# One 512-column matmul for the high and low parts of 256 tokens, and a gate/up evacuation in two pieces

## The chip, the cores and the metric

The kernel runs on one core of a Trainium2 chip. The metric is the device time of one launch in microseconds; the time before is the median of three runs.

The engines are named as the profile names them: PE is TensorE (PEld its weight loads), DVE is VectorE, ACT is ScalarE, POOL is GpSimd, SP the engine that issues the transfers. ps is a tile of PSUM, one bank of 512 float32 columns; blk, t, u, raw, whi and wlo are tiles in SBUF.

## The reference

Two transformer blocks on 256 tokens of 1024 features, in float32:

- Block 1: a modulation from a condition vector, RMS norm, one wide input projection, two attentions (sliding window and block), gates, an output projection, and an MLP `y = square(relu(h @ w_mlp_in)) @ w_mlp_out` of 4096 features, both with a gated residual.
- Block 2: 16 learned tokens are put in front (272 tokens). Layer 0: half a swiglu, a pooling mixer, half a swiglu. Layer 1, whose queries are the 256 tokens alone: half a swiglu, latent attention over shared keys and values, half a swiglu, and a last norm. A swiglu is

```python
def swiglu(h, w_gate, w_up, w_down):
    return (jax.nn.silu(h @ w_gate) * (h @ w_up)) @ w_down
```

with 2816 features between. So there are four swiglus: two of 272 tokens (layer 0) and two of 256 tokens (layer 1).

## The kernel before, in words

Activations are held with features on the 128 partitions and tokens along the columns. A matmul takes a 128 x 128 tile of weights as the stationary operand and streams the token columns.

**Precision.** Weights and activations are float32, each split exactly into two parts of the matmul type float32r: a high part and the rest. `mm3` (L116) makes one product of three matmuls: high weights by high activations (L119), high weights by low activations (L120), low weights by high activations (L121). Each loads its own stationary tile, so the high weights are loaded twice.

**Weights.** `ld` (L82) brings 1 MB (128 x 2048) by one transfer into one of three `raw` buffers and splits it in two halves of 1024 columns: the high part is a copy on ACT (L103), the low part a subtraction on DVE (L104). There are four `whi` and four `wlo` buffers of 1024 columns, so two loads are held at a time, and a split waits until PE is through with the buffer that it takes.

**Projections.** `proj` (L223) takes two feature tiles by step, with k over 8 input tiles: 2 x 8 x 3 matmuls. A step of a swiglu's gate/up projection makes one gate tile and one up tile of the 22. Behind each step its `evac` runs; the first steps' evacuations wait for the norm of the tokens. `down` (L628) is the second projection: four pairs of output tiles, each pair over all k (32 in the MLP, 22 in a swiglu), then `evac` for both.

**Evacuations.** In a swiglu (`ffn`, L689) `evac` (L696) scales the gate by the token norm (DVE, L698), applies Silu (ACT, L699), scales up (DVE, L701), multiplies the two (POOL, L702), and `split_act` takes the high part (ACT, L192) and the low part (DVE, L193). `devac` (L708) adds half of the result to the residual (DVE, L712) and calls what follows: `post_y` (L722) splits the sum for the next projection (L188, L189) and squares it for the norm (POOL, L200, L201). The last swiglu's `post_out` (L1068) makes a scaled copy on ACT (L1069) that PE transposes for the output. The MLP's evacuations are `mlp_evac` (L595) and `mlp_out_evac` (L646).

**Buffers.** High and low parts of an activation are separate tiles of eight features each, from one pool of 13 blocks. `PT` (L468, L999) are three buffers of 384 columns that the attentions use. PSUM has eight banks; a step takes two.

**Order.** Each engine works strictly in the order in which its instructions were emitted. That order is set by a scheduler of the framework, which goes by the order of the program and by its own estimate of when an instruction is ready; the kernel pins it at a few places (`issue_after`).

The 256-column products through `mm3` are: the block-1 projections, the MLP's down projection, and in layer 1 both swiglus, the query projections and the attention's output projection. The MLP's first projection has 258 columns (two carry the shift), layer 0 has 272.

Of the kernel before, what the change touches and what calls it, by code (L numbers as in the profile page):

```python
# [18 lines left out]
S = 256  # L19
# [10 lines left out]
# columns of the packed per-feature vectors  # L30
# [15 lines left out]
def net(ctx, tc, d):  # L46
# [35 lines left out]
    def ld(src, n, sub=1024, spare=False, pool=False, cut=False, steps=None, after=((), ())):  # L82
        """parts of a weight block; with steps, the part behind the first is left to a call of what is put there"""
        raw = wp.tile([128, 2048], F32, tag="raw", name=nm("raw"), bufs=3)
        for a, b in ((0, sub), (sub, n)) if cut else ((0, n),):
            with behind(order[:1]):
                i = nc.sync.dma_start(raw[:, a:b], src[:, a:b])
            if order:
                order[:1] = [i]
        parts = []  # L90
        if spare:
            bh, bl = blk([128, 2048], F32R), blk([128, 2048], F32R)

        def part(a):
            m = min(sub, n - a)
            if spare:
                hi, lo = bh[:, a:a + m], bl[:, a:a + m]
            else:
                hi = wp.tile([128, 1024], F32R, tag="whi", name=nm("whi"), bufs=4)
                lo = wp.tile([128, 1024], F32R, tag="wlo", name=nm("wlo"), bufs=4)  # L100
            e = G if pool and a else V
            with behind(after[a > 0]):
                i = A.activation(hi[:, :m], raw[:, a:a + m], AF.Copy)  # L103
                e.tensor_tensor(lo[:, :m], raw[:, a:a + m], hi[:, :m].bitcast(F32), op=OP.subtract)  # L104
            if order and not a:
                order[1:] = [i]
            parts.append((hi, lo))

        for a in range(0, n, sub):
            if a and steps is not None:  # L110
                steps.append(lambda a=a: part(a))
            else:
                part(a)
        return parts

    def mm3(out, w, c0, xh, xl, start, stop, m=128):  # L116
        """out += (whi + wlo).T (xhi + xlo), the weights stationary."""
        hi, lo = w
        TE.matmul(out, hi[:, c0:c0 + m], xh, start=start, stop=False, skip_group_check=True)  # L119
        TE.matmul(out, hi[:, c0:c0 + m], xl, start=False, stop=False, skip_group_check=True)  # L120
        TE.matmul(out, lo[:, c0:c0 + m], xh, start=False, stop=stop, skip_group_check=True)  # L121

# [88 lines left out]
    def sumsq_late(parts, src, f, n, sumsq=sumsq):  # L211
        """as sumsq, the last two tiles on their own: their squares are ready sooner."""
# [10 lines left out]
    def proj(src, evac, nj, n, yh, yl, first=2, hooks=(), at={}, orders=(range(0, 6), range(6, KD)), spare=(),  # L223
             after={}):
        """two feature tiles by step. The first steps take the tiles of y in the given order, with what is ready
        first in front; the hooks go behind each part of the order and behind the steps that follow, and only
        then the first sums are used. at[j] goes behind step j."""
        hooks = list(hooks)
        waiting = []

# [7 lines left out]
        def mms(pp, w, ks, tiles=(0, 1)):  # L238
            for k in ks:
                for i in tiles:  # L240
                    mm3(pp[i][:, 0:n], w[k // 4], (k % 4) * 256 + i * 128, yh[:, k, :], yl[:, k, :],
                        k == 0, k == KD - 1)
# [7 lines left out]
        for ks in orders:  # L250
# [7 lines left out]
            if len(orders) == 2:  # L258
                if ks[-1] == KD - 1:
                    waiting += [lambda j=j: evac(j, *pps[j]) for j in range(first)]  # L260
                hook()
        tight = len(orders) != 2
        if tight:
            waiting += [lambda j=j: evac(j, *pps[j]) for j in range(first)]
            hook()
        for j in range(first, nj):
            w = ld(src[j], 2048)
            if tight and j == first:
# [5 lines left out]
                evac(j, *pp)  # L274
# [3 lines left out]
            if waiting:  # L278
                waiting.append(lambda j=j, pp=pp: evac(j, *pp))
                hook()  # L280
            else:
                evac(j, *pp)
            if j in at:
                at[j]()

# [7 lines left out]
    def ada(ch, t0, t1, early=False):  # L293
        """feature tiles t0, t1 of the modulation: a row of ada_w.T per partition, times silu(c), summed."""
# [12 lines left out]
    def ada_rest(n, early=False):  # L307
        """n more chunks: gate1, scale2, shift2, gate2."""
# [22 lines left out]
    # position bias with its masks, as a Toeplitz table  # L331
# [50 lines left out]
    # q feature tiles (tokens back to front within each half), then k  # L382
# [25 lines left out]
    def scores(fam, half):  # L408
# [22 lines left out]
        if fam == 0:  # L431
            # heads i, i+4, i+1, i+5 of the sinks
# [24 lines left out]
    def values(fam, heads, Sb, rd, mid):  # L457
        PTs, po = [], []

        def tr(j):  # L460
# [7 lines left out]
            PTs.append(work([128, 384], "PT", bufs=3))  # L468
# [74 lines left out]
    # branches, merge  # L543
# [19 lines left out]
    # out projection, residual; y = x1 * g2 * (1 + scale2), with shift2 as two more columns  # L563
# [27 lines left out]
    # MLP  # L591
    ah = [blk([128, 8, S], F32R) for _ in range(4)]
    al = [blk([128, 8, S], F32R) for _ in range(4)]

    def mlp_evac(f, p):  # L595
# [8 lines left out]
        h = ah[f // 8][:, f % 8, :]  # L604
        A.activation(h, u, AF.Square)
        V.tensor_tensor(al[f // 8][:, f % 8, :], q, h.bitcast(F32), op=OP.subtract)
# [6 lines left out]
    # MLP out, residual; final norm of block 1 and first norm of block 2 both applied late  # L613
# [14 lines left out]
    def down(src, kcs, evac, n, ah, al, before=None):  # L628
        for dp in range(4):
# [3 lines left out]
            for c, (k0, nk) in enumerate(kcs):  # L633
                w = ld(src(dp, c), nk * 256)
                for kk in range(nk):
                    k = k0 + kk
                    for i in range(2):
                        mm3(pp[i][:, 0:n], w[kk // 4], (kk % 4) * 256 + i * 128, ah[k // 8][:, k % 8, :],
                            al[k // 8][:, k % 8, :], k == 0, k == kcs[-1][0] + kcs[-1][1] - 1)
# [6 lines left out]
    def mlp_out_evac(f, p):  # L646
        x2 = work([128, PADW], "t")[:, :S]
        V.scalar_tensor_tensor(x2, p[:, 0:S], mod[:, GA2 + f:GA2 + f + 1], x1[:, f, :], op0=OP.mult, op1=OP.add)
# [6 lines left out]
    down(lambda dp, c: d["mlp_out"][dp * 4 + c], [(8 * c, 8) for c in range(4)], mlp_out_evac, S, ah, al,  # L655
# [17 lines left out]
    def rms_of(get, tiles, n):  # L673
        """hooks that leave the norm of y's tokens in a row."""
# [14 lines left out]
    def ffn(idx, yh, yl, rms, h, n, c0, post, kv=False, before=None, **kw):  # L689
        """h[:, c0:] + half of the swiglu of y; post(f, h_f) for each feature tile of the sum."""  # L690
        gh = [blk([128, nk, n], F32R) for _, nk in FC]
        gl = [blk([128, nk, n], F32R) for _, nk in FC]
        hooks, rc = rms
        c1 = T - n if kv else 0

        def evac(f, pg, pu):  # L696
            g = work([128, PADW], "t")[:, :n]
# [10 lines left out]
        def devac(f, p):  # L708
            if f == 0:
                out.append(blk([128, KD, n]))  # L710
            hn = out[0]
            split[:] = [V.scalar_tensor_tensor(hn[:, f, :], p[:, 0:n], 0.5, h[:, f, c0:], op0=OP.mult, op1=OP.add)]  # L712
            post(f, hn[:, f, :])
# [5 lines left out]
    def make_y(n, y):  # L719
        y += [blk([128, KD, n], F32R), blk([128, KD, n], F32R), newss()[:, :n]]  # L720

    def post_y(y, g, n, late=False, sumsq=sumsq):  # L722
        def post(f, hf):
            if f == 0:
                make_y(n, y)
                if late:
                    y[2] = [y[2]]
            split.append(split_scaled(y[0][:, f, :], y[1][:, f, :], hf, vc(g[0], g[1] + f)))
# [6 lines left out]
    # layer 0  # L735
# [25 lines left out]
    def window(g, w, l0, l1, E):  # L761
        """sums over 2, 4, 8, 16 tokens back"""
# [41 lines left out]
    def post_kv(f, hf):  # L804
        if f == 0:
            make_y(S, y)
            make_y(T, ykv)
        split_scaled(y[0][:, f, :], y[1][:, f, :], hf[:, NM:], vc("ffn1_norm", 8 + f))
# [8 lines left out]
    # shared keys and values  # L817
# [76 lines left out]
    # layer 1  # L894
# [93 lines left out]
    def mla_values(b, Pb, rd):  # L988
        PTs = []
        po = ps()  # L990
        for j in range(2):
# [7 lines left out]
            PT = work([128, 384], "PT", bufs=3)  # L999
# [18 lines left out]
    p3 = post_y(y3, ("ffn2_norm", 8), S)  # L1018
# [20 lines left out]
    # the queries' norms and the scale go with the exponentials  # L1039
# [61 lines left out]
def _layout(i):  # L1101
# [15 lines left out]
    def pairs(w):  # L1117
        """[K, F] -> [F / 256, 128, (K / 128) * 256]"""
# [3 lines left out]
    def tiles(w, c):  # L1122
        """[K, F] -> [128, (F / c) * (K / 128) * c]"""
# [78 lines left out]
```

## Time and profile before

| | before |
|---|---|
| median of three runs | 1280.07 us (1280.05 to 1280.92) |
| profiled execution, first to last instruction | 1279.0 us |
| matmuls | 9908 |
| PE busy | 1240.4 us, 97% |
| DVE busy | 855.1 us, 67% |
| ACT busy | 611.3 us, 48% |
| POOL busy | 363.7 us, 28% |
| read from memory | 236.01 MB |

The profile is of one execution; it gives the span, and the time of a run has the start and the end of the launch beside it, which is not listed. Matmuls are pipelined: the duration of one reaches into the next, so the rate of a stream is read from the distance between two starts.

### The profile page before, as it was taken

Reading aid. Unit: us, or ns where it says so; the run is one execution under the profiler, and the core shown is the slowest. Engines: PE = TensorE matmul, PEld = TensorE weight load, DVE = VectorE, ACT = ScalarE, POOL = GpSimd, SP = SyncE. Lnnn points to the kernel's source line nnn. Section 1 sums busy time; section 2 is a strip of 40 time slices with the busy share of each in tenths; the row PEclk is TensorE's granted clock in tenths of the full one; section 3 lists DMA queues with packets and bytes.
Section 4 is the critical chain, followed back from the end, with each engine's and each line's share of the span. In section 5 each row is a group of like instructions: output and inputs, shape, how many; then the busy total and the mean of one; then the engine's idle time right before and its main releaser. Section 6 shows DMA issues by size and latency. Waiting matters only on the chain.

```text
span 1279.0 us, 24155 instructions
## 1 busy us (share of the span) xinstructions
PE 1240.4 (97%) x9908; PEld 1213.6 (95%) x9908; DVE 855.1 (67%) x1322; ACT 611.3 (48%) x971; POOL 363.7 (28%) x351
## 2 busy tenths in 40 slices
PE   6999999999999999998899999999999999999997
PEld 4988999999999999998899999999999977999997
DVE  7978778887755766566866666666656577666543
ACT  3366445665444544443444444454444454544442
POOL 4333135331325222223222212222222235222221
PEclk9999999999999999999999999999999999999999
DMA  8957864556664554451455455455555423555551
GB/s 326 331 187 285 307 226 169 198 176 253 210 219 165 168 188 173 159 206 65 165 182 181 165 178 168 166 199 170 193 181 182 132 100 129 183 183 189 169 185 53
DMA packets 37057, 238.63 MB, mean 187 GB/s; under 512 B 4242, under 2 KB 6738, under 8 KB 11731
## 3 DMA queue, kind: packets, MB, share of 16 engines
q1 hardware_dynamic: 36946, 237.10, 52.9%
q8 instruction: 77, 1.26, 0.4%
q14 instruction: 34, 0.27, 0.1%
HBM read 236.01 MB, written 1.07 MB: 185 GB/s over the span
## 4 chain that ended last, share of the span: by engine, by line
PE 86%; DVE 7%; issue 3%; POOL 2%; ACT 2%; POOLq 0%; DVEq 0%; ACTq 0%
PE ps L121 27%; PE ps L120 27%; PE ps L119 27%; DVE wlo L104 2%; DVE blk L302 1%; DVE blk L189 1%; POOL blk L341 1%; DVE blk L768 1%; POOL t L561 1%; PE ps L477 1%; PE ps L150 1%; PE ps L467 0%; ACT whi L103 0%; PE ps L175 0%; PE ps L523 0%
## 5 line engine op out<-in xcount | busy, mean ns | idle before, releaser
L121 PE MATMUL ps<-blk,wlo 128*128 128x256 f32 (+2 forms) x3080 | 878.3, 286 | 9.6 <-DVE wlo L104 6.2
L120 PE MATMUL ps<-blk,whi 128*128 128x256 f32 (+2 forms) x3080 | 879.4, 286 | 2.9 <-DVE blk L361 1.8
L119 PE MATMUL ps<-blk,whi 128*128 128x256 f32 (+2 forms) x3080 | 871.1, 286 | 7.6 <-ACT blk L188 4.3
L104 DVE TENSOR_TENSOR wlo<-raw,whi 128x1024 fp32r<-128x1024 f32 (+2 forms) x395 | 485.8, 1233 | 248.0 <-ACT whi L103 247.5
L121 PEld LDWEIGHTS ps<-blk,wlo 128*128 128x128 f32 x3080 | 588.3, 191 | 11.8 <-DVE wlo L104 7.4
L119 PEld LDWEIGHTS ps<-blk,whi 128*128 128x128 f32 x3080 | 585.8, 192 | 10.0 <-ACT blk L188 4.5
L120 PEld LDWEIGHTS ps<-blk,whi 128*128 128x128 f32 x3080 | 588.6, 191 | 3.8 <-DVE blk L361 2.3
L103 ACT ACTIVATE whi<-raw 128x1024 fp32r<-128x1024 f32 (+3 forms) x403 | 412.5, 1030 | 364.4 <-PE ps L120 339.3
L702 POOL TENSOR_TENSOR u<-u,t 128x272 f32<-128x272 f32 (+1 forms) x88 | 117.5, 1336 | 349.0 <-ACT t L699 344.7
L192 ACT ACTIVATE blk<-u 128x272 fp32r<-128x272 f32 (+1 forms) x88 | 37.2, 424 | 129.6 <-POOL u L702 129.6
L193 DVE TENSOR_TENSOR blk<-u,blk 128x272 fp32r<-128x272 f32 (+1 forms) x88 | 39.1, 446 | 83.5 <-ACT blk L192 83.5
L200 POOL TENSOR_TENSOR sq<-blk 128x256 f32<-128x256 f32 (+1 forms) x45 | 36.7, 817 | 129.1 <-DVE blk L712 124.8
L201 POOL TENSOR_TENSOR ss<-ss,sq 128x256 f32<-128x256 f32 (+1 forms) x52 | 64.5, 1243 | 3.5
L698 DVE TENSOR_TENSOR t<-ps,R 128x272 f32<-128x272 f32 (+1 forms) x88 | 37.8, 429 | 10.4 <-POOL u L702 5.9
L603 POOL TENSOR_TENSOR q<-u 128x256 f32<-128x256 f32 x32 | 28.3, 901 | 54.6 <-ACT u L601 54.2
L189 DVE SCALAR_TENSOR_TENSOR blk<-blk,vec,blk 128x272 fp32r<-128x272 f32 (+1 forms) x48 | 38.4, 844 | 0.2 <-ACT blk L188 0.2
L699 ACT ACTIVATE t<-t 128x272 f32<-128x272 f32 (+1 forms) x88 | 35.8, 410 | 5.3 <-DVE t L698 4.9
L701 DVE TENSOR_TENSOR u<-ps,R 128x272 f32<-128x272 f32 (+1 forms) x88 | 37.8, 429 | 0.1
L302 DVE SCALAR_TENSOR_TENSOR raw<-raw,csb 128x1024 f32<-128x1024 f32 x30 | 36.8, 1250 | 1.5 <-DMA raw<-in_ada_w 1.5
L168 POOL TENSOR_TENSOR col<-col,mhalf 128x2 f32<-128x2 f32 (+1 forms) x12 | 12.2, 1020 | 80.5 <-DVE col L161 70.8
L188 ACT ACTIVATE blk<-blk,vec 128x272 fp32r<-128x272 f32 (+1 forms) x48 | 22.1, 507 | 26.1 <-DVE blk L774 14.0
L302 DVE SCALAR_TENSOR_TENSOR blk<-blk,csb 128x1024 f32<-128x1024 f32 x18 | 32.0, 1813 | 1.4 <-DMA blk<-in_ada_w 1.4
(213 smaller groups left out, 695.5 us busy)
## 6 DMA issues: line engine op xcount, KB each, us to landing
raw<-in_f_gu SPq DMA_DIRECT2D x88, 1024.0 KB, 4.9
raw<-in_f_down SPq DMA_DIRECT2D x32, 1024.0 KB, 4.9
raw<-in_mlp_in SPq DMA_DIRECT2D x16, 1024.0 KB, 4.9
raw<-in_mlp_out SPq DMA_DIRECT2D x16, 1024.0 KB, 5.3
raw<-in_ada_w SPq DMA_DIRECT2D x15, 1024.0 KB, 5.1
raw<-in_f_down SPq DMA_DIRECT2D x16, 768.0 KB, 4.3
blk<-in_ada_w SPq DMA_DIRECT2D x9, 1024.0 KB, 8.9
raw<-in_w_gate SPq DMA_DIRECT2D x7, 1024.0 KB, 5.0
```

The lines of the kernel that those rows point to most:

```text
L103: i = A.activation(hi[:, :m], raw[:, a:a + m], AF.Copy)
L104: e.tensor_tensor(lo[:, :m], raw[:, a:a + m], hi[:, :m].bitcast(F32), op=OP.subtract)
L119: TE.matmul(out, hi[:, c0:c0 + m], xh, start=start, stop=False, skip_group_check=True)
L120: TE.matmul(out, hi[:, c0:c0 + m], xl, start=False, stop=False, skip_group_check=True)
L121: TE.matmul(out, lo[:, c0:c0 + m], xh, start=False, stop=stop, skip_group_check=True)
L189: return V.scalar_tensor_tensor(lo, src, g, hi.bitcast(F32), op0=OP.mult, op1=OP.subtract)
L193: V.tensor_tensor(lo, src, hi.bitcast(F32), op=OP.subtract)
L201: G.tensor_tensor(ss, ss, q, op=OP.add)
L302: V.scalar_tensor_tensor(w, w, 1.0, csb, op0=OP.mult, op1=OP.mult, accum_out=mod[:, t:t + 1])
L698: V.tensor_tensor(g, pg[:, 0:n], rc["R"][:, c1:], op=OP.mult)
L701: V.tensor_tensor(u, pu[:, 0:n], rc["R"][:, c1:], op=OP.mult)
L702: G.tensor_tensor(u, u, g, op=OP.mult)
```

## The change

`mm2` and `Parts` are new. A `Parts` tile holds, for each k, the 256 columns of the high part and right behind them the 256 of the low part. `mm2` passes both through the high weights as one matmul of 512 columns into a whole PSUM bank, and the high part through the low weights as one of 256 columns into the bank's first half. The product is then the sum of the two halves of the bank, which the evacuation adds. This is used in the MLP's down projection and in both swiglus of layer 1; all else stays with `mm3`. The gate/up evacuation there is `evac2`: the first piece scales both halves and adds them, the second piece (Silu, product, split) is returned and called by `proj` behind the next step.

```diff
+    def mm2(p, w, c0, x, k, start, stop):
+        hi, lo = w
+        TE.matmul(p[:, 0:2 * S], hi[:, c0:c0 + 128], x.both(k), start=start, stop=False, skip_group_check=True)
+        TE.matmul(p[:, 0:S], lo[:, c0:c0 + 128], x.hi(k), start=False, stop=stop, skip_group_check=True)
+
+    class Parts:
+        def __init__(self, nk):
+            self.t = [blk([128, min(4, nk - k), 2, S], F32R) for k in range(0, nk, 4)]
+        def hi(self, k):
+            return self.t[k // 4][:, k % 4, 0, :]
+        def lo(self, k):
+            return self.t[k // 4][:, k % 4, 1, :]
+        def both(self, k):
+            return self.t[k // 4][:, k % 4].rearrange("p a n -> p (a n)")
...
     def proj(...)
+        late = []
+        def ev(j, pp):
+            for e in late:
+                e()
+            late[:] = [e for e in (evac(j, *pp),) if e]
...
+                    if yl is None:
+                        mm2(pp[i], w[k // 4], c0, yh, k, k == 0, k == KD - 1)
+                    else:
+                        mm3(pp[i][:, 0:n], w[k // 4], c0, yh[:, k, :], yl[:, k, :], k == 0, k == KD - 1)
...
-                evac(j, *pp)
+                ev(j, pp)
...
+        for e in late:
+            e()
...
-            PTs.append(work([128, 384], "PT", bufs=3))
+            PTs.append(work([128, 2 * S], "PT", bufs=4)[:, 0:384])
...
-    ah = [blk([128, 8, S], F32R) for _ in range(4)]
-    al = [blk([128, 8, S], F32R) for _ in range(4)]
+    am = Parts(32)
...
     def mlp_out_evac(f, p):
         x2 = work([128, PADW], "t")[:, :S]
-        V.scalar_tensor_tensor(x2, p[:, 0:S], mod[:, GA2 + f:GA2 + f + 1], x1[:, f, :], op0=OP.mult, op1=OP.add)
+        x2l = work([128, PADW], "u")[:, :S]
+        ga = mod[:, GA2 + f:GA2 + f + 1]
+        A.activation(x2l, p[:, S:2 * S], AF.Copy, scale=ga)
+        V.scalar_tensor_tensor(x2, p[:, 0:S], ga, x1[:, f, :], op0=OP.mult, op1=OP.add)
+        V.tensor_tensor(x2, x2, x2l, op=OP.add)
...
     def ffn(idx, yh, yl, rms, h, n, c0, post, kv=False, before=None, **kw):
+        two = yl is None
+        if two:
+            gh, gl = Parts(22), None
...
+        def evac2(f, pg, pu):
+            Rb = rc["R"][:, None, c1:].to_broadcast([128, 2, S])
+            g2 = work([128, 2 * S], "PT", bufs=4).rearrange("p (a n) -> p a n", a=2)
+            V.tensor_tensor(g2, pg.rearrange("p (a n) -> p a n", a=2), Rb, op=OP.mult)
+            u2 = work([128, 2 * S], "PT", bufs=4).rearrange("p (a n) -> p a n", a=2)
+            V.tensor_tensor(u2, pu.rearrange("p (a n) -> p a n", a=2), Rb, op=OP.mult)
+            g = work([128, PADW], "t")[:, :n]
+            G.tensor_tensor(g, g2[:, 0], g2[:, 1], op=OP.add)
+            u = work([128, PADW], "u")[:, :n]
+            G.tensor_tensor(u, u2[:, 0], u2[:, 1], op=OP.add)
+            def second():
+                A.activation(g, g, AF.Silu)
+                G.tensor_tensor(u, u, g, op=OP.mult)
+                split_act(gh.hi(f), gh.lo(f), u)
+            return second
...
         def devac(f, p):
+            if two:
+                b = work([128, PADW], "u")[:, :n]
+                A.activation(b, p[:, n:2 * n], AF.Copy, scale=0.5)
             split[:] = [V.scalar_tensor_tensor(hn[:, f, :], p[:, 0:n], 0.5, h[:, f, c0:], op0=OP.mult, op1=OP.add)]
+            if two:
+                V.tensor_tensor(hn[:, f, :], hn[:, f, :], b, op=OP.add)
             post(f, hn[:, f, :])
```

`down`, `make_y`, `post_y` and `post_kv` take the new layout in the same way; `mlp_evac` writes its parts to `am`.

## Rows read from the trace of the kernel before

**Rows 1.** The page: busy time, share of the span, instructions.
```profile
PE 1240.4 (97%) x9908; PEld 1213.6 (95%) x9908; DVE 855.1 (67%) x1322; ACT 611.3 (48%) x971; POOL 363.7 (28%) x351
```
**Rows 2.** Windows: length, busy PE, PEld, DVE, ACT, POOL, clock, DMA share, GB/s.
```profile
1038.80:1042.40 3.60, 3.60 (x17) 2.94 (x16) 3.48 (x16) 2.63 (x11) 0.04 (x1) 1.00 0.00 0
...
810.00:1019.00 209.00, 209.00 (x1742) 209.00 (x1741) 129.91 (x173) 98.68 (x142) 49.61 (x44) 1.00 0.53 179
304.00:396.00 92.00, 92.00 (x767) 92.00 (x765) 58.54 (x66) 39.53 (x48) 30.34 (x30) 1.00 0.60 216
```
**Rows 3.** Groups by shape, PE: count, busy us, mean ns, idle before and releaser.
```profile
L121 PE MATMUL ps<-blk,wlo 128*128 128x256 f32 x1752 | 497.0, 285 | 8.8 <-DVE wlo L104 5.4 <-POOL wlo L104 3.3
...
L119 PE MATMUL ps<-blk,whi 128*128 128x256 f32 x1752 | 492.6, 286 | 2.9 <-ACT blk L358 2.8
```
**Rows 4.** Timeline of PE, 256 columns: start us, duration, line; first and last of 19.
```profile
1149.75 0.28 PE L121 MATMUL ps<-blk,wlo 128*128 128x256 f32 x1
...
1151.91 0.28 PE L121 MATMUL ps<-blk,wlo 128*128 128x256 f32 x1
```
**Rows 5.** Timeline of PE, 512 columns, first and last of 17.
```profile
1038.78 0.40 PE L890 MATMUL ps<-wlo,blk 128*128 128x512 f32 x1
...
1042.48 0.40 PE L891 MATMUL ps<-whi,blk 128*128 128x512 f32 x1
```
**Rows 6.** Timeline of PE, 320 columns, first and last of 32.
```profile
74.39 0.31 PE L524 MATMUL ps<-whi,blk 128*128 128x320 f32 x1
...
78.93 0.31 PE L522 MATMUL ps<-whi,blk 128*128 128x320 f32 x1
```
**Rows 7.** Timeline of PE, 272 columns, first and last of 18.
```profile
499.82 0.28 PE L119 MATMUL ps<-blk,whi 128*128 128x272 f32 x1
...
501.94 0.29 PE L121 MATMUL ps<-blk,wlo 128*128 128x272 f32 x1
```
**Rows 8.** Timeline of DVE in layer 1's last gate/up projection.
```profile
1107.95 0.42 DVE L698 TENSOR_TENSOR t<-ps,R 128x256 f32<-128x256 f32 x1
...
1109.35 1.23 DVE L104 TENSOR_TENSOR wlo<-raw,whi 128x1024 fp32r<-128x1024 f32 x1 [0.61 <-ACT whi L103]
1111.65 0.42 DVE L193 TENSOR_TENSOR blk<-u,blk 128x256 fp32r<-128x256 f32 x1 [1.08 <-ACT blk L192]
1112.60 1.23 DVE L104 TENSOR_TENSOR wlo<-raw,whi 128x1024 fp32r<-128x1024 f32 x1 [0.52 <-ACT whi L103]
1113.75 0.42 DVE L698 TENSOR_TENSOR t<-ps,R 128x256 f32<-128x256 f32 x1
```
**Rows 9.** Timeline of ACT there; in brackets the wait before and its releaser.
```profile
1108.25 1.06 ACT L103 ACTIVATE whi<-raw 128x1024 fp32r<-128x1024 f32 x1 [1.51 <-PE ps L120]
1109.22 0.40 ACT L699 ACTIVATE t<-t 128x256 f32<-128x256 f32 x1
1111.20 0.42 ACT L192 ACTIVATE blk<-u 128x256 fp32r<-128x256 f32 x1 [1.59 <-POOL u L702]
1111.53 1.04 ACT L103 ACTIVATE whi<-raw 128x1024 fp32r<-128x1024 f32 x1
```
**Rows 10.** Timeline of POOL, layer 1's first and last gate/up projections.
```profile
825.44 0.74 POOL L702 TENSOR_TENSOR u<-u,t 128x256 f32<-128x256 f32 x1 [4.77 <-ACT t L699]
...
1109.75 1.42 POOL L702 TENSOR_TENSOR u<-u,t 128x256 f32<-128x256 f32 x1 [4.40 <-ACT t L699]
```
**Rows 11.** Timeline of DVE and ACT at the end.
```profile
1269.23 0.79 DVE L712 SCALAR_TENSOR_TENSOR blk<-ps,blk 128x256 f32<-128x256 f32 x2 [8.42 <-PE ps L121]
...
1273.40 1.41 DVE L1090 TENSOR_SCALAR blk<-ps,col 128x512 f32<-128x512 f32 x2 [0.82 <-POOL col L168]
...
1269.69 0.51 ACT L1069 ACTIVATE blk<-blk,vec 128x256 f32<-128x256 f32 x1 [9.61 <-DVE blk L712]
```
**Rows 12.** Timeline of POOL and PE where the first swiglu's norm is summed.
```profile
394.05 0.74 POOL L201 TENSOR_TENSOR ss<-ss,sq 128x256 f32<-128x256 f32 x1
...
395.61 0.61 PE L150 MATMUL ps<-ones,ss 128*128 128x4 f32 x5
```

More of the change, by code (lines that the diff above doesn't have):

```diff
@@ L240, in mms @@
                 for i in tiles:
-                    mm3(pp[i][:, 0:n], w[k // 4], (k % 4) * 256 + i * 128, yh[:, k, :], yl[:, k, :],
-                        k == 0, k == KD - 1)
+                    c0 = (k % 4) * 256 + i * 128
+                    if yl is None:
+                        mm2(pp[i], w[k // 4], c0, yh, k, k == 0, k == KD - 1)
+                    else:
+                        mm3(pp[i][:, 0:n], w[k // 4], c0, yh[:, k, :], yl[:, k, :], k == 0, k == KD - 1)
         ws, steps = [], []
@@ L259, in proj @@
                 if ks[-1] == KD - 1:
-                    waiting += [lambda j=j: evac(j, *pps[j]) for j in range(first)]
+                    waiting += [lambda j=j: ev(j, pps[j]) for j in range(first)]
                 hook()
@@ L263, in proj @@
         if tight:
-            waiting += [lambda j=j: evac(j, *pps[j]) for j in range(first)]
+            waiting += [lambda j=j: ev(j, pps[j]) for j in range(first)]
             hook()
@@ L278, in proj @@
             if waiting:
-                waiting.append(lambda j=j, pp=pp: evac(j, *pp))
+                waiting.append(lambda j=j, pp=pp: ev(j, pp))
                 hook()
             else:
-                evac(j, *pp)
+                ev(j, pp)
             if j in at:
                 at[j]()
+        for e in late:
+            e()
     nc.sync.dma_start(oneh, d["onehot"])
@@ L603, in mlp_evac @@
         G.tensor_tensor(q, u, u, op=OP.mult)
-        h = ah[f // 8][:, f % 8, :]
+        h = am.hi(f)
         A.activation(h, u, AF.Square)
-        V.tensor_tensor(al[f // 8][:, f % 8, :], q, h.bitcast(F32), op=OP.subtract)
+        V.tensor_tensor(am.lo(f), q, h.bitcast(F32), op=OP.subtract)
     Rm = []
@@ L626, in net, with down @@
     G.tensor_copy(h0[:, :, 0:NM], meta)
-    def down(src, kcs, evac, n, ah, al, before=None):
+    def down(src, kcs, evac, n, ah, al=None, before=None):
         for dp in range(4):
@@ L636, in down @@
                     k = k0 + kk
+                    last = k == kcs[-1][0] + kcs[-1][1] - 1
                     for i in range(2):
-                        mm3(pp[i][:, 0:n], w[kk // 4], (kk % 4) * 256 + i * 128, ah[k // 8][:, k % 8, :],
-                            al[k // 8][:, k % 8, :], k == 0, k == kcs[-1][0] + kcs[-1][1] - 1)
+                        c0 = (kk % 4) * 256 + i * 128
+                        if al is None:
+                            mm2(pp[i], w[kk // 4], c0, ah, k, k == 0, last)
+                        else:
+                            mm3(pp[i][:, 0:n], w[kk // 4], c0, ah[k // 8][:, k % 8, :], al[k // 8][:, k % 8, :],
+                                k == 0, last)
             for i in range(2):
@@ L653, in mlp_out_evac @@
         sumsq(ss2[:, NM:T], xg, f == 0, S)
-    down(lambda dp, c: d["mlp_out"][dp * 4 + c], [(8 * c, 8) for c in range(4)], mlp_out_evac, S, ah, al,
+    down(lambda dp, c: d["mlp_out"][dp * 4 + c], [(8 * c, 8) for c in range(4)], mlp_out_evac, S, am,
          before=lambda dp: ada_rest(1))
@@ L689, in ffn @@
     def ffn(idx, yh, yl, rms, h, n, c0, post, kv=False, before=None, **kw):
-        gh = [blk([128, nk, n], F32R) for _, nk in FC]
-        gl = [blk([128, nk, n], F32R) for _, nk in FC]
+        two = yl is None
+        if two:
+            gh, gl = Parts(22), None
+        else:
+            gh = [blk([128, nk, n], F32R) for _, nk in FC]
+            gl = [blk([128, nk, n], F32R) for _, nk in FC]
         hooks, rc = rms
         c1 = T - n if kv else 0
+        def evac2(f, pg, pu):
[13 more added lines that the diff above has]
+            return second
         def evac(f, pg, pu):
+            if two:
+                return evac2(f, pg, pu)
             g = work([128, PADW], "t")[:, :n]
@@ L711, in devac @@
             hn = out[0]
+            if two:
+                b = work([128, PADW], "u")[:, :n]
+                A.activation(b, p[:, n:2 * n], AF.Copy, scale=0.5)
             split[:] = [V.scalar_tensor_tensor(hn[:, f, :], p[:, 0:n], 0.5, h[:, f, c0:], op0=OP.mult, op1=OP.add)]
+            if two:
+                V.tensor_tensor(hn[:, f, :], hn[:, f, :], b, op=OP.add)
             post(f, hn[:, f, :])
@@ L717, in ffn, with make_y, post_y @@
         return out[0]
-    def make_y(n, y):
-        y += [blk([128, KD, n], F32R), blk([128, KD, n], F32R), newss()[:, :n]]
-    def post_y(y, g, n, late=False, sumsq=sumsq):
+    def make_y(n, y, parts=False):
+        if parts:
+            y += [Parts(KD), None, newss()[:, :n]]
+        else:
+            y += [blk([128, KD, n], F32R), blk([128, KD, n], F32R), newss()[:, :n]]
+    def post_y(y, g, n, late=False, sumsq=sumsq, parts=False):
         def post(f, hf):
             if f == 0:
-                make_y(n, y)
+                make_y(n, y, parts)
                 if late:
                     y[2] = [y[2]]
-            split.append(split_scaled(y[0][:, f, :], y[1][:, f, :], hf, vc(g[0], g[1] + f)))
+            yh, yl = (y[0].hi(f), y[0].lo(f)) if parts else (y[0][:, f, :], y[1][:, f, :])
+            split.append(split_scaled(yh, yl, hf, vc(g[0], g[1] + f)))
             if late:
@@ L805, in post_kv @@
         if f == 0:
-            make_y(S, y)
+            make_y(S, y, True)
             make_y(T, ykv)
-        split_scaled(y[0][:, f, :], y[1][:, f, :], hf[:, NM:], vc("ffn1_norm", 8 + f))
+        split_scaled(y[0].hi(f), y[0].lo(f), hf[:, NM:], vc("ffn1_norm", 8 + f))
         split_scaled(ykv[0][:, f, :], ykv[1][:, f, :], hf, vc("kv_in", f))
@@ L998, in mla_values @@
             TE.transpose(p[:, 256:384], Pb[:, j, 288:416], ident)
-            PT = work([128, 384], "PT", bufs=3)
+            PT = work([128, 2 * S], "PT", bufs=4)[:, 0:384]
             A.copy(PT, p[:, 0:384])
@@ L1017, in net @@
     y3 = []
-    p3 = post_y(y3, ("ffn2_norm", 8), S)
+    p3 = post_y(y3, ("ffn2_norm", 8), S, parts=True)
     h5 = blk([128, KD, S])
```

## The prediction

> **What bounds the kernel now.** I read the busy times first, then the stages, then TensorE's shapes, then one step of a stage on every engine. TensorE is busy for 1240.4 of 1279.0 us [rows 1], so the first question is which matmuls the change touches and whether TensorE ever waits there. The table by stage answers the second half: in the MLP's down projection (304 to 396 us) and in the first swiglu of layer 1 (810 to 1019 us) TensorE is busy in every microsecond, at a granted clock of 1.00, which is its upper level, 2.4 GHz; VectorE is busy 62 to 64% there, GpSimd 24 to 33%, the DMA engines 53 to 60% [rows 2]. In these stages the time is the number of matmuls times the distance from one start to the next. The busy mean of one (285 ns) is not that distance, because matmuls overlap [rows 3]; the distance has to be read from the starts.
>
> **The matmuls.** The change goes only where an activation has 256 tokens and stays in two parts through `Parts`: the MLP's down projection (4 x 32 x 2 = 256 units of one weight tile by one k), and the two swiglus of layer 1, each with 22 x 8 x 2 = 352 units of gate/up and 4 x 22 x 2 = 176 of down. Together 256 + 2 x 528 = 1312 units, of the 1752 that the 256-column form has [rows 3]; the 258- and 272-column stages stay as they are. A unit is now three 256-column matmuls and becomes one of 512 and one of 256: the columns stay 768, one matmul and one weight load go.
>
> 256 columns: 19 starts in a row, 2.16 us over 18 distances, 120.0 ns [rows 4]. 512 columns occur once, in `vals` (L889 to L891), in the same type and into a whole PSUM bank like the new one: 17 starts, 3.70 us over 16, 231.3 ns [rows 5], at clock 1.00 [rows 2]. So a unit goes from 360.0 to 351.3 ns, 8.7 less, and 1312 units give **-11.5 us**. The bounds come from the two neighbouring widths. From 256 to 320 columns (32 starts, 4.54 us over 31, 146.5 ns [rows 6]) a column costs 0.414 ns, which leaves 14.0 ns per matmul that don't depend on its width: if 512 followed that line, the gain would be 18.4 us. From 272 (18 starts, 2.12 us over 17, 124.7 ns [rows 7]) to 512 a column costs 0.444 ns, which leaves only 3.9 ns: 5.1 us. I take the value between, since it is the one with the very shape; what no row shows is 512 and 256 in alternation.
>
> A rule speaks against it. The Trainium skill (TensorE: Matmul & The Clock Gate, section "Back-to-back issue gap") gives for one stream of matmuls columns / 2.4 GHz plus 2.5 ns; by that the removed matmul is worth 2.5 ns and all units 3.3 us. The rows do not bear out its 109.2 ns for 256 columns.
>
> **Gate/up evacuation.** Before, a step of layer 1 cost VectorE two weight subtractions of 1.23, two 256-column scalings of 0.42 (L698, L701) and the low part of 0.42: 3.72 us [rows 8]; ScalarE two copies of 1.06, the Silu 0.40, the high part 0.42: 2.94 [rows 9]; GpSimd one product. After, VectorE's two scalings read 512 columns: about 0.75 each, from the 512-column PSUM reads at the end (two in 1.41 [rows 11]); its sum is 2 x 1.23 + 2 x 0.75 + 0.42 = 4.38. GpSimd gets two adds besides the product. One such instruction takes 0.74 alone and 1.42 beside a weight subtraction [rows 10], so three are 2.2 to 4.3 us. ScalarE stays at 2.94. The new step is 16 units = 5.62 us, so all three stay below TensorE, and the cost is taken as **0**. The cover is the lead of the weight parts: four pairs of high/low buffers of half a step each, so a split that starts when TensorE releases a buffer has three half steps, 3 x 2.81 = 8.4 us, less its own 1.06 + 1.23: 6.1 us of slack. Behind a waiting evacuation stand just these splits on ScalarE and VectorE; TensorE waits only if they come more than 6.1 us late. If the sum on VectorE passed 5.62, every step would pay the excess. The eight PSUM banks are no limit: a step takes two, and they are free once both scalings have read them. The sum on GpSimd ties the second piece to the first; with a step between, nobody on TensorE waits for it before the last k of the down projection, some 15 us on (44 units).
>
> **Down evacuation.** Each of 8 feature tiles in three stages gets one ScalarE read of the second half (about 0.4, as L192 [rows 9]) beside the existing VectorE step, and one VectorE add (0.42, as L193 [rows 8]). Inside a stage 15 us lie between two evacuations, so they cost 0. At the ends:
> - MLP down to the first swiglu: the pair's chain of squares on GpSimd ends at 394.79, TensorE's sums follow at 395.61 [rows 12]. The adds delay its start by 0.4 to 0.75 us, the slack is 0.82: **0**, at worst +0.3.
> - Layer 1's first swiglu to the query projection: 54 matmuls over k below 6 (3 x 6 x 3 x 0.120 = 6.5 us) stand before k 6 and 7 are wanted; the extra is under 1 us: **0**.
> - The last swiglu to the output: nothing covers. The pair's two VectorE steps take 0.79 and ScalarE's scaled copy starts after the first, 0.46 us behind [rows 11]. With the second step likely issued ahead of the first add (it needs no other engine), that copy starts 0.75 us later, and everything behind it: **+0.75**, between 0.4 and 1.2.
>
> **The rest.** `PT` buffers go from 3 to 4 of 512 columns, which can only let a transposed copy of attention start sooner: 0. No transfer is added or moved on SP's or GpSimd's queue, and the weights' 1 MB per step now has 5.62 us in place of 5.76 at a DMA share of 0.53 [rows 2]: 0. `Parts` only lays high and low side by side; the number of 13 shared blocks held is the same. A first matmul now needs the low part too; at the starts of these stages the tiles 0 to 5 are long there: 0.
>
> **Sum.** -11.5 + 0.75 = -10.7 us against the span of 1279.0, so 1268.3. The median of the runs is 1280.07, 1.1 us above this span (start and end of the launch lie around it), so the forecast is **1269.3 us**. With the bounds: -18.4 + 0.4 gives 1262.1; -5.1 + 1.3 gives 1276.3.
>
> **Rivals.**
> A. *A matmul has little fixed cost.* 3.9 ns by the line from 272 to 512: -5.1 + 0.75, 1275.7 us. For it: 272 columns cost only 4.7 ns more than 256. Against: 256 and 320 agree on 14. By the rule of the Trainium skill above the time would be 1277.5. Chance 0.10.
> B. *Slower: a loop through the queues.* In the rows of before, ScalarE takes the high part (1111.20) ahead of the next weight copy (1111.53), and VectorE takes the weight subtraction (1112.60) ahead of the scaling (1113.75) [rows 8, 9]. If the planner that orders each engine keeps that, a step must wait for: two scalings (2 x 0.66 from start to start), the other weight subtraction that GpSimd sits out (1.15), add and product (2 x 0.74), high part 0.42, weight copy 1.06, subtraction 1.15 = 6.6, about 6.7 with handoffs, against 5.62. It decides as soon as this loop is longer than the step: 1.1 x 44 steps = 48 us, less two leads of 6.1 = +36, less the 10.7: about 1305 us. For it: this order is the present one, and ScalarE's high part already sits behind a product of 1.42 [rows 10]. Against: the high part now comes over 1 us later than half a step (2.81), so that the weight copy should be ready first, and then the loop opens. Chance 0.11.
> C. *VectorE becomes the bound.* If each weight subtraction also waits once for a GpSimd add of 0.74, VectorE's step is 4.38 + 1.48 = 5.86: 0.24 x 44 = 10.6 us, which eats the gain: 1280 us. For it: 1.24 us of a step is all the idle that it has left. Against: the first add falls under the second scaling, which reads PSUM. Chance 0.09.
> That the pieces do not come apart (the planner may issue the second as soon as its inputs are there) changes nothing in the sum: TensorE does not wait for either.
>
> **The numbers.** The forecast has 0.70. About 0.2% (2.6 us) is what a measurement tells from no change. Faster: 0.70 and most of A, 0.77; same: C and the rest of A, 0.12; slower: B, 0.11. The range goes from 1263 (nearly the line of 256 and 320) to 1277 (A and the page's rule), and leaves out B and C.
>
> **What would show it.** Right: 2624 matmuls in these units where 3936 were; 512-column starts 231 ns and 256-column ones 120 ns apart; the first swiglu of layer 1 shorter by 352 + 176 units x 8.7 = 4.6 us, the MLP's down by 2.2; TensorE without idle in both; the end, from the last matmul of the units, longer by under 1 us. Wrong: idle on TensorE put down to a weight subtraction, every step, in gate/up only (B, C); or a unit near 356 ns (A) or 346 (the line of 256 and 320) in place of 351.

## The result, and the profile after

The change made the kernel slower: 1298.12 us median (1297.63 to 1298.82, four runs) against 1280.32, a ratio of 1.0142 with a 95% interval of 1.0128 to 1.0157. The forecast was 1269.3.

| | before | after |
|---|---|---|
| median | 1280.32 us | 1298.12 us |
| profiled execution: its time / its span | not listed / 1279.0 | 1297.63 / 1295.5 |
| matmuls | 9908 | 8596 |
| PE busy | 1240.4 us | 1236.9 us |
| POOL busy | 363.7 us | 444.0 us |

The matmuls went as the change says: the groups by shape (count, busy us, mean ns, idle before with its releaser) have 1312 of 512 columns (L126) and 1312 of 256 (L127), and 440 units are left to `mm3` of the 1752 in [rows 3].

```profile
L126 PE MATMUL ps<-blk,whi 128*128 128x512 f32 x1312 | 465.5, 398 | 0.0
L127 PE MATMUL ps<-blk,wlo 128*128 128x256 f32 x1312 | 372.3, 284 | 21.8 <-DVE wlo L104 21.8
```

Their price is in the timeline of PE, here in the MLP's down projection: six units from one start of a 512-column matmul to another.

```profile
339.84 0.40 PE L126 MATMUL ps<-blk,whi 128*128 128x512 f32 x1
...
341.96 0.40 PE L126 MATMUL ps<-blk,whi 128*128 128x512 f32 x1
```

2.12 us over 6 is 353 ns a unit, where it was 3 x 120.0 [rows 4]: 6.7 ns less, so by this price the matmuls became some 8.8 us faster in all. The loss is elsewhere, and the list of what PE waited for has only one new line: the weights' low part, 30 times.

```profile
PE ps L127 <- DVE wlo L104: 21.8, 30, 2.5
```

One of the 30, of 2.5 us, comes at the start of the second swiglu and was there before, under L121. The other 29 come once a step, 14 in the first swiglu and 15 in the second. Two of them, in PE's timeline:

```profile
1149.15 0.39 PE L127 MATMUL ps<-blk,wlo 128*128 128x256 f32 x1 [0.75 <-DVE wlo L104]
1155.72 0.39 PE L127 MATMUL ps<-blk,wlo 128*128 128x256 f32 x1 [0.66 <-DVE wlo L104]
```

The table by stage puts that into layer 1's two swiglus. PE was busy throughout 810 to 1019 us before [rows 2] and idle for 2.6 us in the second swiglu (first row here, of the kernel before); now it is idle for 9.9 us in the first swiglu and 11.9 in the second (second and third row), while DVE and POOL are far from full (67% and 41%, 63% and 43%). Columns: length, busy PE, PEld, DVE, ACT, POOL, clock, DMA share, GB/s.

```profile
1066.00:1269.50 203.50, 200.95 (x1662) 200.74 (x1661) 119.18 (x159) 91.69 (x129) 55.81 (x49) 0.99 0.46 156
...
807.00:1018.00 211.00, 201.15 (x1158) 173.73 (x1158) 141.97 (x174) 97.47 (x147) 86.47 (x84) 1.00 0.48 168
1080.00:1285.50 205.50, 193.58 (x1071) 164.29 (x1070) 128.79 (x154) 88.27 (x128) 87.72 (x87) 0.99 0.44 154
```

The busy PE there is an overestimate, as matmuls that overlap a wait still count: a wait shows as 0.65 to 0.76 us, and the step is longer by 0.92 (below). One step of gate/up shows the rest. DVE's timeline:

```profile
1116.16 0.68 DVE L744 TENSOR_TENSOR PT<-ps,R 128x512 f32<-128x512 f32 x1
1116.76 0.68 DVE L746 TENSOR_TENSOR PT<-ps,R 128x512 f32<-128x512 f32 x1
1117.36 1.38 DVE L104 TENSOR_TENSOR wlo<-raw,whi 128x1024 fp32r<-128x1024 f32 x1
1120.64 0.42 DVE L214 TENSOR_TENSOR blk<-u,blk 128x256 fp32r<-128x256 f32 x1 [1.90 <-ACT blk L213]
1121.59 1.23 DVE L104 TENSOR_TENSOR wlo<-raw,whi 128x1024 fp32r<-128x1024 f32 x1 [0.52 <-ACT whi L103]
1122.73 0.68 DVE L744 TENSOR_TENSOR PT<-ps,R 128x512 f32<-128x512 f32 x1
```

ACT's and POOL's in the same step:

```profile
1117.70 0.42 ACT L753 ACTIVATE t<-t 128x256 f32<-128x256 f32 x1 [1.76 <-POOL t L748]
1120.19 0.42 ACT L213 ACTIVATE blk<-u 128x256 fp32r<-128x256 f32 x1 [2.07 <-POOL u L754]
1120.51 1.99 ACT L103 ACTIVATE whi<-raw 128x1024 fp32r<-128x1024 f32 x2
...
1116.92 0.74 POOL L748 TENSOR_TENSOR t<-PT 128x256 f32<-128x256 f32 x1 [3.34 <-DVE PT L744]
1117.61 1.73 POOL L750 TENSOR_TENSOR u<-PT 128x256 f32<-128x256 f32 x1
1119.42 0.74 POOL L754 TENSOR_TENSOR u<-u,t 128x256 f32<-128x256 f32 x1
```

Read it as a circle. The two scalings end at 1117.44. POOL's second add needs the second scaling, but DVE has gone on to a weight subtraction, and the add takes 1.73 us in place of 0.74. The product follows, then the high part on ACT (1120.19), which the queue holds ahead of both weight copies (1120.51); the first copy releases the weight subtraction (1121.59), and only behind that does DVE take the next step's scaling (1122.73). From scaling to scaling it is 6.57 us, and nothing in it waits for PE. PE's own step is 16 x 0.353 = 5.65 us. Before, a weight copy said that it had waited for PE [rows 9]; in these steps none does. The low part of a tile (1120.64) also comes ahead of the next step's scaling: the two pieces that the code calls a step apart run in one step.

### The profile page after: what moved, and what is told of

Read it like the earlier page. It is cut to its first block, busy times and chain, and to the rows that moved or that the text cites. A ratio compares the mean times of both kernels' runs of the same rounds, so it can differ in the third digit from the quotient of the medians.

```text
span 1295.5 us, 21678 instructions
## 1 busy us (share of the span) xinstructions
PE 1236.9 (95%) x8596; PEld 1141.8 (88%) x8596; DVE 893.9 (69%) x1346; ACT 617.1 (48%) x995; POOL 444.0 (34%) x439
## 4 chain that ended last, share of the span: by engine, by line
PE 66%; DVE 11%; POOL 10%; issue 7%; ACT 5%; DVEq 0%; ACTq 0%; POOLq 0%
PE ps L120 15%; PE ps L121 15%; PE ps L119 14%; PE ps L126 12%; PE ps L127 6%; POOL u L750 5%; ACT whi L103 3%; DVE wlo L104 3%; POOL u L754 2%; DVE blk L335 2%; POOL t L748 2%; DVE PT L744 2%; DVE blk L210 1%; POOL t L594 1%; DVE blk L842 1%
## 5 line engine op out<-in xcount | busy, mean ns | idle before, releaser
L104 DVE TENSOR_TENSOR wlo<-raw,whi 128x1024 fp32r<-128x1024 f32 (+2 forms) x395 | 492.4, 1251 | 193.6 <-ACT whi L103 192.6
L121 PE MATMUL ps<-blk,wlo 128*128 128x272 f32 (+2 forms) x1768 | 505.7, 288 | 7.6 <-DVE wlo L104 4.7
L120 PE MATMUL ps<-blk,whi 128*128 128x272 f32 (+2 forms) x1768 | 507.2, 288 | 2.9 <-DVE blk L394 1.8
L119 PE MATMUL ps<-blk,whi 128*128 128x272 f32 (+2 forms) x1768 | 497.7, 287 | 7.6 <-ACT blk L209 4.3
L126 PE MATMUL ps<-blk,whi 128*128 128x512 f32 x1312 | 465.5, 398 | 0.0
L127 PE MATMUL ps<-blk,wlo 128*128 128x256 f32 x1312 | 372.3, 284 | 21.8 <-DVE wlo L104 21.8
L121 PEld LDWEIGHTS ps<-blk,wlo 128*128 128x128 f32 x1768 | 336.2, 190 | 9.7 <-DVE wlo L104 5.6
L119 PEld LDWEIGHTS ps<-blk,whi 128*128 128x128 f32 x1768 | 333.3, 191 | 10.0 <-ACT blk L209 4.5
L120 PEld LDWEIGHTS ps<-blk,whi 128*128 128x128 f32 x1768 | 336.5, 190 | 3.8 <-DVE blk L394 2.3
L126 PEld LDWEIGHTS ps<-blk,whi 128*128 128x128 f32 x1312 | 247.1, 188 | 58.4 <-DVE blk L210 0.2
L127 PEld LDWEIGHTS ps<-blk,wlo 128*128 128x128 f32 x1312 | 248.6, 189 | 31.6 <-DVE wlo L104 31.6
L767 POOL TENSOR_TENSOR u<-u,t 128x272 f32<-128x272 f32 x44 | 58.4, 1328 | 168.8 <-ACT t L764 164.5
L748 POOL TENSOR_TENSOR t<-PT 128x256 f32<-128x256 f32 x44 | 33.7, 766 | 136.8 <-DVE PT L744 136.8
L750 POOL TENSOR_TENSOR u<-PT 128x256 f32<-128x256 f32 x44 | 72.2, 1641 | 0.0
L753 ACT ACTIVATE t<-t 128x256 f32<-128x256 f32 x44 | 18.3, 419 | 70.0 <-POOL t L748 70.0
```

The lines of the kernel that those rows point to most:

```text
L126: TE.matmul(p[:, 0:2 * S], hi[:, c0:c0 + 128], x.both(k), start=start, stop=False, skip_group_check=True)
L127: TE.matmul(p[:, 0:S], lo[:, c0:c0 + 128], x.hi(k), start=False, stop=stop, skip_group_check=True)
L748: G.tensor_tensor(g, g2[:, 0], g2[:, 1], op=OP.add)
L750: G.tensor_tensor(u, u2[:, 0], u2[:, 1], op=OP.add)
L767: G.tensor_tensor(u, u, g, op=OP.mult)
```

## The experiments

The theory after the profile is this **loop**: the order in the queues of ACT and DVE ties one step's evacuation to the next step's weights, and the circle is longer than PE's step. The rival is **load**: two more adds on POOL and wider scalings on DVE fill these two, whatever their order. A third is that the down projections are part of it.

**Pinning the second piece.** The second piece is kept back three steps in the program and queued behind the first weight split of that step, on ACT and on DVE. `firsts` holds the first copy and the first subtraction of the latest `ld`.

```diff
...
         for j in range(first, nj):
             w = ld(src[j], 2048)
+            while late and late[0][0] <= j - 3:
+                with behind(firsts):
+                    late.pop(0)[1]()
...
```

> The changed kernel with one thing more: the second piece of a gate/up evacuation (Silu, product, high part, low part) is queued on ScalarE and VectorE behind the first split of the weights of three steps later, so that a weight copy no longer stands behind a high part that waits for GpSimd. Loop theory (the slowdown is a chain through the queues of 6.57 us a step, longer than TensorE's 16 units): the gate/up steps fall to TensorE's pace, 16 x 0.353 = 5.65 us; 1312 units save 6.6 ns each = 8.7 us, the end costs 0.6: about 1272 us. Load theory (VectorE and GpSimd are full, two adds a step on a shared way to SBUF): the order is not what counts, 1293 us or more.

1272.82 us, ratio 0.9940 (0.9928 to 0.9953) to the kernel before. The table by stage for 1130 to 1230 us, of the slow kernel and then of this one (columns as above):

```profile
1130.00:1230.00 100.00, 91.22 (x499) 75.95 (x498) 63.76 (x77) 41.41 (x61) 48.70 (x47) 1.00 0.44 155
```

```profile
1130.00:1230.00 100.00, 100.00 (x569) 86.67 (x568) 72.34 (x81) 46.94 (x68) 55.05 (x44) 1.00 0.54 183
```

In this kernel's timeline, DVE's rows and then ACT's, a weight copy waits for PE again:

```profile
1133.48 0.68 DVE L749 TENSOR_TENSOR PT<-ps,R 128x512 f32<-128x512 f32 x1
1134.08 0.68 DVE L751 TENSOR_TENSOR PT<-ps,R 128x512 f32<-128x512 f32 x1
1134.68 3.07 DVE L106 TENSOR_TENSOR wlo<-raw,whi 128x1024 fp32r<-128x1024 f32 x2
1138.83 0.42 DVE L218 TENSOR_TENSOR blk<-u,blk 128x256 fp32r<-128x256 f32 x1 [1.08 <-ACT blk L217]
1139.17 0.68 DVE L749 TENSOR_TENSOR PT<-ps,R 128x512 f32<-128x512 f32 x1
...
1133.01 1.05 ACT L105 ACTIVATE whi<-raw 128x1024 fp32r<-128x1024 f32 x1
1134.30 1.06 ACT L105 ACTIVATE whi<-raw 128x1024 fp32r<-128x1024 f32 x1 [0.24 <-PE ps L130]
```

The same work on the same engines in another order takes 25.3 us less. Load falls: in the same 100 us PE is busy throughout, with DVE and POOL busier (72% and 55%) than in the slow kernel (64% and 49%).

**Pinning on DVE alone.** `firsts[1:]` is the subtraction without the copy.

```diff
-                with behind(firsts):
+                with behind(firsts[1:]):
```

> As the kernel with the second piece pinned, but pinned on VectorE alone: ScalarE keeps the high part ahead of both weight copies. Loop theory: the chain still closes through ScalarE's queue (two scalings 1.2, subtraction that blocks the add 1.2, add and product 1.5, high part 0.4, copy 1.0, subtraction 1.15), so about 6.5 us a step and about 1298 us. If VectorE's order were what counts: about 1272 us.

1304.92 us (two runs), 1.0191 (1.0173 to 1.0210). DVE's order is the pinned one, ACT's is not, and the circle is there, even longer:

```profile
1133.01 0.42 DVE L218 TENSOR_TENSOR blk<-u,blk 128x256 fp32r<-128x256 f32 x1
1133.34 0.69 DVE L749 TENSOR_TENSOR PT<-ps,R 128x512 f32<-128x512 f32 x1
...
1140.25 0.69 DVE L749 TENSOR_TENSOR PT<-ps,R 128x512 f32<-128x512 f32 x1
...
1137.37 0.42 ACT L217 ACTIVATE blk<-u 128x256 fp32r<-128x256 f32 x1 [2.07 <-POOL u L759]
1137.70 2.00 ACT L105 ACTIVATE whi<-raw 128x1024 fp32r<-128x1024 f32 x2
```

6.91 us a step: 6.57 and the 0.33 of a low part that now stands between the subtraction and the scaling, inside the circle. So it is ACT's queue, the high part ahead of the weight copies, that closes it; an order on DVE alone does not open it. An order on ACT alone was not tried.

**One add less.** The up product takes the high half alone.

```diff
-            G.tensor_tensor(u, u2[:, 0], u2[:, 1], op=OP.add)
...
-                G.tensor_tensor(u, u, g, op=OP.mult)
+                G.tensor_tensor(u, u2[:, 0], g, op=OP.mult)
```

> The changed kernel without the add of the up product's two halves (the part from the low activations is left out there). Loop theory: the chain loses one GpSimd instruction and the wait behind the weight subtraction; from one scaling to the next 1.2 + 0.74 + wait 0.2 + 0.42 + 1.0 + 0.1 + 1.15 + handoffs is 5.6 to 5.8 us, next to TensorE's 5.65, so 1272 to 1278 us. Load theory: VectorE keeps 4.4 us a step and meets two GpSimd instructions in place of three, 1285 us or more.

1270.59 us, 0.9923 (0.9910 to 0.9937), though the queues have the order of the slow kernel.

```profile
1134.02 0.68 DVE L744 TENSOR_TENSOR PT<-ps,R 128x512 f32<-128x512 f32 x1
...
1139.86 0.68 DVE L744 TENSOR_TENSOR PT<-ps,R 128x512 f32<-128x512 f32 x1
```

5.84 us: this circle is still longer than 5.65, by 0.19, and 20 steps of that are 3.8 us, which the lead of the weight parts covers: of the waits for a low part on L127 one is left, the 2.5 us that was there before. It was under my range by 1.4 us. In this profile the pairs of the last swiglu take 347 ns and not 353 (last section), which is 3.5 us for its 528 units and enough to account for that; PE's step is then 5.55 us there, and the lead covers the larger excess too.

**The down projections alone.** Gate/up of layer 1 goes back to `mm3` and the one-piece evacuation, on the new layout.

```diff
                     if yl is None:
-                        mm2(pp[i], w[k // 4], c0, yh, k, k == 0, k == KD - 1)
+                        mm3(pp[i][:, 0:n], w[k // 4], c0, yh.hi(k), yh.lo(k), k == 0, k == KD - 1)
...
-            if two:
-                return evac2(f, pg, pu)
...
```

> The change in the three down projections alone; gate/up of layer 1 goes back to three matmuls and its evacuation in one piece. 256 + 352 = 608 units at 6.6 ns less are 4.0 us, the end costs 0.6: about 1277 us, with gate/up steps of 5.76 us as before. If the down projections or their evacuations were part of the loss, it would be over 1280.

1275.54 us, 0.9963 (0.9949 to 0.9976). The three down projections are sound: they gain 4.9 us, with an interval of 3.1 to 6.5, which takes in the 3.4 expected.

**The low part behind the next scalings.** In the pinned kernel DVE still has a circle of 5.69 us, above: scalings, the second add behind one subtraction, the product behind the other, high part, low part, scaling. Here the low part moves out of it; `scaled2[f + 1:f + 2]` is the second scaling of the next step.

```diff
...
-                split_act(gh.hi(f), gh.lo(f), u)
+                with behind(scaled2[f + 1:f + 2]):
+                    split_act(gh.hi(f), gh.lo(f), u)
```

> As the kernel pinned on both engines, and the low part of a tile is queued on VectorE behind the next step's scalings. In the pinned run VectorE's own chain (two scalings, the add behind one subtraction, the product behind the other, high part, low part, next scaling) took 5.69 us, just over TensorE's 5.65. Loop theory: without it the steps run at TensorE's 5.65 and only the two last of each gate/up stay at 6.6; the lead covers those, so 1270 to 1273 us, at most 2 us under the pinned run. Load theory: no difference, or slower because VectorE waits more often.

1270.76 us, 0.9926 (0.9911 to 0.9941). It beats both kernels, and is 2.1 us under the pinned one by the medians, which their intervals do not separate. Nor is it shown that the gap comes from DVE's circle: PE was busy throughout in the pinned kernel's steps too, and in the last swiglu a pair takes 353 ns in the pinned kernel's profile and 347 in this one's (last section). For 528 units that is 3.5 us, about what the two spans differ by (1272.0 and 1268.7). DVE now waits for PE:

```profile
1135.93 0.69 DVE L750 TENSOR_TENSOR PT<-ps,R 128x512 f32<-128x512 f32 x1 [0.22 <-PE ps L131]
1136.54 0.68 DVE L752 TENSOR_TENSOR PT<-ps,R 128x512 f32<-128x512 f32 x1
1137.74 1.47 DVE L106 TENSOR_TENSOR wlo<-raw,whi 128x1024 fp32r<-128x1024 f32 x1 [0.52 <-ACT whi L105]
1139.14 0.41 DVE L218 TENSOR_TENSOR blk<-u,blk 128x256 fp32r<-128x256 f32 x1
1140.03 1.23 DVE L106 TENSOR_TENSOR wlo<-raw,whi 128x1024 fp32r<-128x1024 f32 x1 [0.48 <-ACT whi L105]
1141.48 0.69 DVE L750 TENSOR_TENSOR PT<-ps,R 128x512 f32<-128x512 f32 x1 [0.22 <-PE ps L131]
```

**The kernel before with a longer circle.** If the loop is the cause, the kernel before must fall in the same way, with none of the new matmuls.

```diff
...
             G.tensor_tensor(u, u, g, op=OP.mult)
+            if n == S:
+                for _ in range(2):
+                    G.tensor_tensor(u, u, one, op=OP.mult)
```

> The kernel before, with two more GpSimd products (by ones) in a row behind each gate/up product of layer 1. TensorE's work, VectorE's and ScalarE's are unchanged. Loop theory: the old chain of 4.9 to 5.1 us a step grows by two times 0.74 to about 6.5, over TensorE's 5.76; 0.75 us x some 40 steps less two leads of 6 us is 15 to 20 us: about 1297 us, scalings 6.5 us apart. If the added columns or TensorE's new mix of shapes were the cause of the slowdown, this stays at 1280.

1311.81 us, 1.0240 (1.0224 to 1.0257): 31 us for 88 small instructions on an engine that was busy 28%. PE's waits from 290 us on, and a step in DVE's and ACT's rows:

```profile
PE ps L121 <- DVE wlo L104: 26.3, 37, 2.5
```

```profile
1134.91 0.42 DVE L700 TENSOR_TENSOR t<-ps,R 128x256 f32<-128x256 f32 x1
...
1141.59 0.42 DVE L700 TENSOR_TENSOR t<-ps,R 128x256 f32<-128x256 f32 x1
...
1139.05 0.42 ACT L194 ACTIVATE blk<-u 128x256 fp32r<-128x256 f32 x1 [3.21 <-POOL u L707]
1139.37 1.99 ACT L103 ACTIVATE whi<-raw 128x1024 fp32r<-128x1024 f32 x2
```

6.68 us a step where PE needs 5.76. The mechanism is the expected one; the sum was too low. The circle is 0.2 longer than I worked out, and 0.92 x 40 = 37 us less the measured 31 leaves only 6 us for both leads together, where I had taken off 12. Where PE waits can be counted in the trace: once a step in 32 steps, 16 in each swiglu, and twice 0.6 us ahead of them, which is 32 x 0.92 + 1.2 = 31 us. Why this kernel starts with less lead was not tried.

**One piece.** The second piece is called at once.

```diff
-            late[:] = [e for e in (evac(j, *pp),) if e]
+            for e in (evac(j, *pp),):
+                if e:
+                    e()
```

> The changed kernel with the second piece called at once, not a step later. The scheduler had already put the second piece into its own step, so the emitted order is nearly the same: 1298 us, scalings 6.57 us apart. If the step between the pieces did anything, this is slower.

1300.50 us (two runs), 1.0155 (1.0135 to 1.0176), scalings 6.57 us apart. The step between the pieces in the program is no step on the chip: in a step of the loop the rows of DVE, ACT and POOL stand in the same order with it and without.

## Why the prediction was wrong

**The step that failed** is "Gate/up evacuation", at the words "the cost is taken as **0**. The cover is the lead of the weight parts". The working compared each engine's sum with the step (4.38, 2.94 and up to 4.3 us against 5.62) and let the lead of 6.1 us hide what came late. The sums are right (DVE's rows above come to 4.39 us), and so is the lead: in the second swiglu the scalings had fallen 5.9 us behind six steps of 5.65 (from 1102.60 to 1142.44) when PE first waited, at 1142.58. Neither is enough: a circle through three queues can be longer than the step while no engine in it is full, and a lead is a stock, spent once, while the circle's excess is paid every step. 6.57 - 5.65 = 0.92 us over some 40 steps is 37 us; less two leads of about 6 that is 25, and the pinned kernel, which differs in order alone, is faster by 25.3. That the two agree so closely is luck. The same sum gives 38 us for the kernel pinned on DVE alone, which is 32.1 slower than the pinned one, and 25 for the longer circle in the kernel before, where 31 was measured. Counted where PE waits, the changed kernel has 29 such steps, 27 us.

**Rival B had it, with the wrong odds.** Its circle of 6.7 us was measured at 6.57, its 1305 us at 1298. I gave it 0.11 because the high part would come later than half a step after the scalings, so that the weight copy "should be ready first, and then the loop opens". It does come late, 4.0 us after the first scaling (1120.19 against 1116.16), but that is the chip's time. The order was fixed beforehand, by the scheduler's own estimate, and stayed that of [rows 9]: high part first. The row already showed a high part that waited 1.59 us for POOL while a weight copy stood behind it, so it was on view that the planned order need not be the order of readiness in just this place; I read that row for the rival and then argued from real durations.

**The other steps, against what they measured.**
- *The matmuls*, -11.5 us: a unit takes 353 ns in most stages, not 351.3, so 8.8. The row in `vals` was the nearest; in alternation the pair costs 2 ns more, and in some stages 5 less (last section). Rival A (356) is not borne out, though 353 lies between 351.3 and it: with the end's 0.6 added, the 4.9 us that the down projections alone gain are 9 ns for each of 608 units (6 at the low end of the interval), where A has 3.9.
- *The rule of the Trainium skill* (TensorE: Matmul & The Clock Gate, section "Back-to-back issue gap"), columns / 2.4 GHz plus 2.5 ns, would give 325 ns for a unit; no row is near it. The same section says that this formula has no budget for the weight loads, and here every matmul has one of its own (8596 of each in the changed kernel).
- *The end*, +0.75 us: from the start of the last matmul of the units to the last instruction it was 9.7 us before (1269.27 to 1279.0) and is 10.4 after (1285.14 to 1295.5), so 0.6. The number came out, the way to it only in part. ACT's read of the first tile's second half does not run beside DVE's first scaling but ahead of it: the row puts the scaling's wait down to that read, and it starts 0.42 us behind it. Both sums do come behind both scalings, and ACT's copy waits for the first of them. That copy starts 1.59 us after the last matmul of the units where it was 0.42 [rows 11], so 1.2 us later and not 0.75; about half of this does not reach the end, which the prediction had not foreseen.

```profile
1285.17 0.73 ACT L779 ACTIVATE u<-ps 128x256 f32<-128x256 f32 x2 [9.02 <-PE ps L127]
1286.73 0.51 ACT L1143 ACTIVATE blk<-blk,vec 128x256 f32<-128x256 f32 x1 [0.82 <-DVE blk L782]
...
1285.59 0.77 DVE L780 SCALAR_TENSOR_TENSOR blk<-ps,blk 128x256 f32<-128x256 f32 x2 [8.43 <-ACT u L779]
1286.28 0.75 DVE L782 TENSOR_TENSOR blk<-blk,u 128x256 f32<-128x256 f32 x2
```

- *The down evacuations*, 0: right as far as the run without the new gate/up tells, which is faster than the kernel before.
- *Rival C* (VectorE is full): wrong. With the order changed DVE does the same work in steps of 5.55 to 5.69 us and has idle left.
- *That the pieces do not come apart* "changes nothing in the sum": the first half is true (they do not), the second is what cost the gain. Had they come apart the circle would have been open, as it is in the pinned kernel, which is what the change meant.

With the order mended, 1270.76 us is 1.5 us from the forecast and within its range. The terms as measured, -8.8 and +0.6, would give 1272; the rest may be the pair's lower price in the last swiglu, which the last section comes to.

## What to carry to other kernels

Beside each engine's sum, add up the circle that the queues close from one step to the next: producer, every instruction that stands ahead of it in an in-order queue, consumer, back to the producer's next turn. If it is longer than the bottleneck's step the difference is paid every step, however idle the engines are, and buffers only delay it. An order in the program is not an order on the engines: look in the trace for which instruction an in-order queue holds ahead of the one that feeds the bottleneck, and pin that one.

## What had not been expected of the hardware

- GpSimd and VectorE keep each other waiting. A 256-column add or product of 0.74 us takes 1.73 when a weight subtraction has started just before it (1117.36 and 1117.61 above): it ends 0.60 us behind the subtraction's end, so most of it comes after that. A product takes 1.60 in the pinned kernel beside the second subtraction. The other way round, a subtraction of 1.23 takes 1.47 where an add had started first (1137.40 on POOL, 1137.74 on DVE, in the run with the low part moved). A scaling that reads PSUM does not hold an add up (1116.92, 0.74 beside the second scaling). 1.0 us of the circle of 6.57 is that wait; without it the circle would be about 5.6 us, an estimate, and no longer than PE's step. [Rows 10] had shown the wait for the product, and rival B had counted it at 1.15; the sum that the forecast rests on had it only in GpSimd's busy time.
- The pair of 512 and 256 columns has two prices. In the MLP's down projection it is 353 ns. In the last swiglu it is 353 in the pinned kernel's profile (six units from 1130.33 to 1132.45) and 347 in the run with the low part moved (six units from 1129.84 to 1131.92), at a granted clock of 1.00 in both; the run with one add less has 347 there too, and the changed kernel has it in the first swiglu's down projection. If the 256-column matmul keeps its 120 ns, the 512-column one takes 233 and 227, near the two values that the rows of before left open (231 in [rows 5], 226 by the line through [rows 4, 6]). 528 units x 6.6 ns are 3.5 us. What decides between them was not tried.

```profile
1130.33 0.40 PE L130 MATMUL ps<-blk,whi 128*128 128x512 f32 x1
...
1132.45 0.40 PE L130 MATMUL ps<-blk,whi 128*128 128x512 f32 x1
```

```profile
1129.84 0.39 PE L130 MATMUL ps<-blk,whi 128*128 128x512 f32 x1
...
1131.92 0.39 PE L130 MATMUL ps<-blk,whi 128*128 128x512 f32 x1
```
